# Two attention heads side by side on half arrays, bfloat16 masks, and one mask product for four mLSTM heads

## The chip, the core and the metric

The kernel runs on one core of one Trainium2 chip. The metric is the device time of one execution in microseconds (us), from three timed runs; one more execution was taken with the hardware profiler. TensorE (PE in the profile) does the matrix products, VectorE (DVE) and ScalarE (ACT) the elementwise work, GpSimd (POOL) and SyncE (SP) here issue transfers.

## What is computed

A batch of one with 256 tokens and 256 context tokens goes through a first block of two trunk layers (each a mixer with differential attention, and a gated feed-forward part) and then a second block (mLSTM in both directions beside a windowed attention with a sink, then a mixture of 16,384 small experts). Three places of the reference matter:

```python
def diff_attend(q, k, v, lam):                      # first block
    s = jnp.einsum('bqhmd,bkhmd->bhmqk', q, k).astype(jnp.float32) * (DIFF_QK ** -0.5)
    p = jax.nn.softmax(s, axis=-1)
    a = p[:, :, 0] - lam * p[:, :, 1]
    return jnp.einsum('bhqk,bkhd->bqhd', a.astype(v.dtype), v)
...
    log_d = jnp.where(seen, log_d, -jnp.inf)        # mLSTM, per head and chunk of 128
    m_t = jnp.maximum(log_inter, jnp.max(log_d, axis=-1))
    s = jnp.einsum('bhctk,bhcsk->bhcts', q, k) * jnp.exp(log_d - m_t[..., None])
...
    s_loc = jnp.where(mask[None, :, None, None], s_loc, -jnp.inf)   # windowed attention, 8 heads of 64
    p = _softmax_with_sink(jnp.concatenate([s_loc, s_ctx], axis=-1), sink_b)
```

## The kernel before, in words

Activations lie feature by token in SBUF. Each large product is written as three products of float32r halves: `weight` (lines 262 to 266) loads a weight tile of 128x1024 through SP into one of three `wraw` buffers, ACT casts it to `whi`, DVE subtracts to `wlo`; `gemm` (line 282) multiplies. One such tile against 256 tokens is 24 products of 256 columns. The order of instructions on each engine is written by a scheduler from the program order, priorities and a cost model; engines then run in that order.

**First block.** `mixer_d` works through steps `(seg, hp, hh, qt)`: queries of the tokens against 512 keys (seg 0) and, in layer 0 alone, queries of the context against 256 keys (seg 1); `hp` is a pair of heads, `hh` the head in it, `qt` a block of 128 queries. Layer 0 has 16 steps, layer 1 has 8. For a step, `scores` (lines 775 to 784) makes two products, two maxima, two exponentials and the weighted difference; `turned` (791, 793) transposes the result by up to four products with the identity into the one `pt` bank and ACT copies it to one of two `aT` buffers; `values` (800) multiplies each block of keys (4 or 2 of them) with the 64 columns of that head's values, writing to the 64 partitions `hh * 64` of `po` (`tile_position=(0, hh * 64)`: the left or the right half of the array's columns). Scores run two steps ahead, and after each step `next(fill)` puts in a piece of `mixer_fm`, the other products of the layer. Line 926 in `mixer_fm` already multiplies with both halves in turn.

**mLSTM.** `weights(tt, dd)`, called four times, builds for four heads a bank `pD`: per head a float32 product of a selector of 4 rows with a row of running maxima (line 1256), then a float32 product of the identity with a mask of 0 and 1e30 (1257). ACT takes four exponentials, DVE multiplies. `outputs` follows one turn later.

**Windowed attention.** `window_attention` has 16 steps `(i, qt, hh)`. `scores` (1382) multiplies 64 rows (a head's features, in partitions `hh * 64`: the upper or lower half of the array's rows) with 512 columns of keys, then adds the window's mask by a float32 product with the identity (1384); DVE takes the maximum (1387, 1388), ACT the exponential and the sink's (1391, 1392), DVE sums, inverts and scales (1393 to 1395). `turned` (1402, 1404) transposes by four products into `pt` and copies. Line 1419 multiplies with the values, in column halves. Scores run two steps ahead, and one of 16 products for the gates fills in after each step as long as there are any (five are used in the mLSTM).

A float32 product shows in the trace as two weight loads (PEld) and two MATMUL records; a float32r or 16-bit product as one of each. `self.att()` has four PSUM banks, `self.acc()` two, `pt` and `po` one each.

Of the kernel before, what the change touches and what calls it, by code (L numbers as in the profile page):

```python
# [11 lines left out]
F32 = mybir.dt.float32  # L12
F32R = mybir.dt.float32r
BF16 = mybir.dt.bfloat16
# [75 lines left out]
def second_constants():  # L90
    k = Pack()
    i = np.arange(P)
    k.add("tri_le", (i[:, None] <= i[None, :]).astype(np.float32))
    k.add("tri_ge", (i[:, None] >= i[None, :]).astype(np.float32))
    k.add("mask_le", np.where(i[:, None] <= i[None, :], 0.0, BIG))
    k.add("mask_ge", np.where(i[:, None] >= i[None, :], 0.0, BIG))
    k.add("win0", np.where(i[None, :] <= i[:, None], 0.0, -BIG))
    k.add("win1", np.where(i[None, :] >= i[:, None], 0.0, -BIG))
# [116 lines left out]
class Kernel:  # L215
# [472 lines left out]
    def mixer_d(self, l, mp, hi, lo, mix, lam, pva, fill, begin, later):  # L688
# [67 lines left out]
        self.lambdas(l, lam)  # L756
        gsub = self.sm([P, 1], "gsub", bufs=1)
        V.tensor_scalar(gsub, self.prm[f"subln{l}"], 1.0 - LAM_INIT[l], None, op0=OP.mult)
        steps = [(seg, hp, hh, qt) for seg in range(2 if full else 1) for hp in range(2) for hh in range(2) for qt in range(2)]
        span = lambda seg: (0, 1, 2, 3) if seg == 0 else (2, 3)  # L760
        ready = {}

        def scores(i):
            seg, hp, hh, qt = steps[i]
            k0, nk = span(seg)[0] * P, len(span(seg)) * P
            if seg and hh + qt == 0:
                for t in range(2):
# [25 lines left out]
            nc.scalar.copy(aT[:, :len(kts), :], pt[:, :len(kts) * P].rearrange("p (j t) -> p j t", t=P))  # L793
            return aT

        def values(i, aT, po):
            seg, hp, hh, qt = steps[i]
            h, kts = hp * 2 + hh, span(seg)
            for j, kt in enumerate(kts):
                nc.tensor.matmul(po[hh * 64:hh * 64 + 64, qt * P:qt * P + P], v[:, kt, h * 64:h * 64 + 64], aT[:, j, :], start=j == 0, stop=j == len(kts) - 1, tile_position=(0, hh * 64))  # L800

        def scaled(seg, ss, o_sb):
            r = self.rsqrt(ss.rearrange("p a b -> p (a b)"), [P, 8], "subr")
# [24 lines left out]
        fill = turns(fill)  # L828
        scores(0)
        scores(1)  # L830
        po, ss, o_sb = None, None, []
        for i, (seg, hp, hh, qt) in enumerate(steps):
            if hh + qt == 0:
                po = self.po()
            if hp + hh + qt == 0:
                ss, o_sb = self.sm([P, 2, 4], "subss", bufs=2), []
            if i == 8:
                later(2)
            aT = turned(i)
            if i + 2 < len(steps):  # L840
                scores(i + 2)
            for _ in range(1 if full else 2):
                next(fill, None)
            values(i, aT, po)
# [197 lines left out]
    def token_mixer(self):  # L1042
# [3 lines left out]
        with ExitStack() as st:  # L1046
# [11 lines left out]
            mT = (self.t(mp, [P, 4, TOK], F32R, "mT_hi"), self.t(mp, [P, 4, TOK], F32R, "mT_lo"))  # L1058
            aT = (self.t(mp, [P, 4, TOK], F32R, "aT_hi"), self.t(mp, [P, 4, TOK], F32R, "aT_lo"))
            ot = self.t(mp, [P, 4, TOK], F32, "o_th")  # L1060
            h = (hi[:, :, :TOK], lo[:, :, :TOK])

            def fm_tile(m):
# [39 lines left out]
    def mlstm(self, lp, mp, hi, lo, fm_tile, ot, mT, fill):  # L1103
# [264 lines left out]
        return kT, qT  # L1368

    def window_attention(self, lp, kT, qT, av, aT, fill):  # L1370
        nc, k, rows = self.nc, self.k, self.rows
        V = nc.vector
        nsink = self.sm([P, 8], "nsink", bufs=1)
        V.tensor_scalar(nsink, rows["sink"], -1.0, None, op0=OP.mult)
        steps = [(i, qt, hh) for i in range(4) for qt in range(2) for hh in range(2)]
        ready = {}

        def scores(n):
            i, qt, hh = steps[n]
            hd, r = i * 2 + hh, hh * 64  # L1380
            ps = self.att()
# [3 lines left out]
            mx = self.sm([P, 1], "wmx")  # L1385
            sk = rows["sink"][:, hd:hd + 1]
            V.tensor_reduce(mx, ps, axis=AX.X, op=OP.max, negate=True)
            V.tensor_tensor(mx, mx, nsink[:, hd:hd + 1], op=OP.min)
            e = self.t(lp, [P, 512], F32, "wexp", 3)
            sm = self.sm([P, 2], "wsm")  # L1390
            nc.scalar.activation(e, ps, AF.Exp, bias=mx, accum_out=sm[:, 0:1])
            nc.scalar.activation(sm[:, 1:2], sk, AF.Exp, bias=mx)
            V.tensor_tensor(sm[:, 0:1], sm[:, 0:1], sm[:, 1:2], op=OP.add)
            V.reciprocal(sm[:, 0:1], sm[:, 0:1])
            V.tensor_scalar(e, e, sm[:, 0:1], None, op0=OP.mult)
            ready[n] = e

        def turned(n):
            e = ready.pop(n)
# [3 lines left out]
            pT = self.t(lp, [P, 4, P], F32, "wpT", 2)  # L1403
            nc.scalar.copy(pT.rearrange("p a b -> p (a b)"), pt)
            return pT

        scores(0)
        scores(1)
        po = None
        for n, (i, qt, hh) in enumerate(steps):  # L1410
            if qt + hh == 0:
                po = self.po()
            pT = turned(n)
            if n + 2 < len(steps):
                scores(n + 2)
# [4 lines left out]
            if qt + hh == 2:  # L1420
                self.split(aT[0][:, i, :], aT[1][:, i, :], po[:, :TOK])
        for _ in fill:
            pass
# [298 lines left out]
```

## Time and profile before

| | |
|---|---|
| three timed runs | 2079.08, 2081.98, 2083.46 us (median 2081.98) |
| the profiled execution | 2075.71 us, of which the span from the first to the last instruction is 2073.9 us |
| instructions | 38449 |
| HBM read | 352.69 MB, 171 GB/s over the span |

Times in the rows further down are microseconds from the start of the span. A timeline row merges neighbours of one kind: its start, the time from the first start to the last end, and the count of records (xN). Ends of matmuls are modelled and overlap the next one, so what a piece of work takes on PE is read from the start of its row to the start of the next row. A row of stretches has the bounds, the length, the busy time (and instructions) of PE, PEld, DVE, ACT and POOL, the granted TensorE clock as a share of full speed, the DMA share and GB/s. A row of groups ends in: busy us, mean ns of one | idle us of the engine before them, and what ended it.

### The profile page before, as it was taken

How to read it: one execution, taken by the hardware profiler on the slowest of the kernel's cores; microseconds unless marked ns; L12 is line 12 of the kernel's file. 1: busy time of each engine (PE TensorE's matmuls, PEld its weight loads, DVE VectorE, ACT ScalarE, POOL GpSimd, SP SyncE). 2: the span in 40 equal slices, each digit the busy share in tenths (PEclk: the TensorE clock that was granted, in tenths of full speed). 3: DMA queues.
4: the chain of work that ended last, by engine and by line, in shares of the span. 5: the costliest groups of instructions: out<-in, count | busy, mean ns of one | idle time of the engine just before them, and what ended most of it. 6: DMA issues, size and time to landing. Idle time of an engine off the chain costs nothing. (4 is left out here: it accounts for less than half of the span.)

```text
span 2073.9 us, 38449 instructions
## 1 busy us (share of the span) xinstructions
PE 2010.9 (97%) x15084; PEld 1822.1 (88%) x15084; DVE 1675.6 (81%) x3484; ACT 987.2 (48%) x1681; POOL 71.0 (3%) x138
## 2 busy tenths in 40 slices
PE   7999999998999999999999999999999999999999
PEld 3777778887888889999798788999999999999999
DVE  5897889876976779987675479988987898898775
ACT  4476343322324856554344455456544444444444
POOL 0100001111110000000000000000000000000000
PEclk9999999999999999999999999999999999999999
DMA  7632346676663347774341253555465565555564
GB/s 284 214 113 70 132 153 213 224 245 221 215 211 122 103 132 257 262 249 132 103 144 61 77 148 123 162 182 166 146 189 187 179 186 186 179 181 191 183 190 157
DMA packets 99029, 356.23 MB, mean 172 GB/s; under 512 B 11296, under 2 KB 12192, under 8 KB 97312
## 3 DMA queue, kind: packets, MB, share of 16 engines
q1 hardware_dynamic: 77616, 279.21, 41.3%
q0 software_dynamic: 19296, 70.98, 10.3%
q10 hardware_dynamic: 1936, 3.59, 0.6%
q8 instruction: 118, 1.93, 0.4%
q14 instruction: 63, 0.52, 0.1%
HBM read 352.69 MB, written 1.05 MB: 171 GB/s over the span
## 5 line engine op out<-in xcount | busy, mean ns | idle before, releaser
L263 ACT CAST whi<-wraw 128x1024 fp32r<-128x1024 f32 (+2 forms) x524 | 537.8, 1028 | 407.0 <-PE pH L282 95.1
L266 DVE TENSOR_TENSOR wlo<-wraw,whi 128x1024 fp32r<-128x1024 f32 (+3 forms) x552 | 626.6, 1138 | 103.1 <-ACT whi L263 99.9
L1534 PE MATMUL out<-w_hi,whi 128*128 128x256 f32 x1024 | 284.0, 277 | 0.2 <-ACT w_hi L272 0.2
L1534 PE MATMUL out<-w_hi,wlo 128*128 128x256 f32 x1024 | 282.5, 276 | 0.0
L1534 PE MATMUL out<-w_lo,whi 128*128 128x256 f32 x1024 | 282.2, 276 | 0.0
L369 DVE SCALAR_TENSOR_TENSOR junk<-adaw,cvec 128x1024 bf16<-128x1024 f32 x192 | 234.4, 1221 | 49.8 <-DMA adaw<-ada_in 48.4
L1534 PEld LDWEIGHTS out<-w_hi,whi 128*128 128x128 f32 x1024 | 192.3, 188 | 0.3 <-ACT w_hi L272 0.3
L1534 PEld LDWEIGHTS out<-w_hi,wlo 128*128 128x128 f32 x1024 | 192.3, 188 | 0.1
L1534 PEld LDWEIGHTS out<-w_lo,whi 128*128 128x128 f32 x1024 | 192.0, 188 | 0.0
L282 PE MATMUL acc<-h_hi,whi 128*128 128x256 f32 (+1 forms) x880 | 169.8, 330 | 11.2 <-DVE xc L646 4.6
L282 PE MATMUL pH<-p_hi,whi 128*128 128x256 f32 x1128 | 160.4, 282 | 3.7 <-ACT act L1465 3.6
L272 ACT CAST w_hi<-act 128x256 fp32r<-128x256 f32 x128 | 51.9, 406 | 232.3 <-PE out L1534 223.8
L282 PE MATMUL acc<-h_lo,whi 128*128 128x256 f32 (+1 forms) x880 | 160.4, 322 | 0.0
L282 PE MATMUL acc<-h_hi,wlo 128*128 128x256 f32 (+1 forms) x880 | 159.3, 320 | 0.2 <-DVE wlo L266 0.2
L282 PEld LDWEIGHTS acc<-h_hi,whi 128*128 128x128 f32 x880 | 132.6, 193 | 27.0 <-issue 5.8
L282 PE MATMUL pH<-p_hi,wlo 128*128 128x256 f32 x1128 | 152.3, 277 | 0.1
L282 PE MATMUL pH<-p_lo,whi 128*128 128x256 f32 x1128 | 152.3, 277 | 0.0
L282 PEld LDWEIGHTS pH<-p_hi,whi 128*128 128x128 f32 x1128 | 140.7, 188 | 5.2 <-ACT act L1465 5.1
L282 PEld LDWEIGHTS acc<-h_hi,wlo 128*128 128x128 f32 x880 | 131.3, 189 | 13.7 <-DVE wlo L266 0.8
L282 PEld LDWEIGHTS acc<-h_lo,whi 128*128 128x128 f32 x880 | 132.0, 191 | 12.2 <-issue 0.3
L282 PEld LDWEIGHTS pH<-p_hi,wlo 128*128 128x128 f32 x1128 | 139.3, 188 | 0.3 <-DVE wlo L266 0.3
L282 PEld LDWEIGHTS pH<-p_lo,whi 128*128 128x128 f32 x1128 | 139.3, 188 | 0.0
(567 smaller groups left out, 3342.4 us busy)
## 6 DMA issues: line engine op xcount, KB each, us to landing
adaw<-ada_in POOLq DMA_DIRECT2D x128, 512.0 KB, 4.3
wraw<-pu_in SPq DMA_DIRECT2D x128, 512.0 KB, 3.5
wraw<-pv_in SPq DMA_DIRECT2D x128, 512.0 KB, 4.0
wraw<-wup_in SPq DMA_DIRECT2D x88, 512.0 KB, 4.4
wraw<-win_fm_in SPq DMA_DIRECT2D x44, 512.0 KB, 3.5
wraw<-wdn_in SPq DMA_DIRECT2D x32, 512.0 KB, 4.6
wraw<-wout_in SPq DMA_DIRECT2D x24, 512.0 KB, 3.6
adan<-ada0n_in SPq DMA_DIRECT2D x8, 1024.0 KB, 15.1
```

Source lines behind the costliest of these rows:

```text
L263: nc.scalar.copy(hi[:, :n], raw[:, :n])
L266: nc.vector.tensor_sub(lo[:, s], raw[:, s], hi[:, s].bitcast(F32))
L272: self.nc.scalar.copy(hi, src)
L282: nc.tensor.matmul(ps, a[:, k, :], b[:, k, :], start=first and j == 0, stop=last and j == len(todo) - 1)
L369: nc.vector.scalar_tensor_tensor(junk, w, 0.5, cv, op0=OP.mult, op1=OP.mult, accum_out=self.ada[key][:, nt:nt + 1])
L1534: nc.tensor.matmul(part(m), x[:, m, :], y, start=False, stop=False)
```

## The change

Four things. (1) In `mixer_d` the steps run as `(seg, hp, qt, hh)`, so that two heads with the same queries follow each other; the products with the values wait for both heads and alternate between the column halves. (2) In `weights` of the mLSTM one bfloat16 product of the identity with the mask, read four times over, covers all four heads; the four selector products follow it. (3) In `window_attention` a step is a pair of heads: score products of 256 columns alternate between the row halves, the masks are bfloat16, products with the values alternate between the column halves; scores run one pair ahead, `wexp` has 4 buffers for 3 and `wpT` 3 for 2. (4) The four float32 masks leave the table of constants (a transfer of 704 KB becomes 448 KB); the bfloat16 ones are made from `tri_le` and `tri_ge` by four DVE operations, and the identity by one ACT copy, at the start of the second block.

```diff
-    k.add("mask_le", np.where(i[:, None] <= i[None, :], 0.0, BIG))
...
-        steps = [(seg, hp, hh, qt) for seg in range(2 if full else 1) for hp in range(2) for hh in range(2) for qt in range(2)]
+        steps = [(seg, hp, qt, hh) for seg in range(2 if full else 1) for hp in range(2) for qt in range(2) for hh in range(2)]
...
-        def values(i, aT, po):
-            seg, hp, hh, qt = steps[i]
-            h, kts = hp * 2 + hh, span(seg)
+        def values(i, aTs, po):
+
+            seg, hp, qt, _ = steps[i]
+            kts = span(seg)
             for j, kt in enumerate(kts):
-                nc.tensor.matmul(po[hh * 64:hh * 64 + 64, qt * P:qt * P + P], v[:, kt, h * 64:h * 64 + 64], aT[:, j, :], start=j == 0, stop=j == len(kts) - 1, tile_position=(0, hh * 64))
+                for hh in range(2):
+                    h = hp * 2 + hh
+                    nc.tensor.matmul(po[hh * 64:hh * 64 + 64, qt * P:qt * P + P], v[:, kt, h * 64:h * 64 + 64], aTs[hh][:, j, :], start=j == 0, stop=j == len(kts) - 1, tile_position=(0, hh * 64))
...
-            aT = turned(i)
+            aTs.append(turned(i))
...
-            values(i, aT, po)
+            if hh == 1:
+                values(i, aTs, po)
+                aTs = []
...
+            k["ident_b"] = self.t(mp, [P, P], BF16, "ident_b")
+            nc.scalar.copy(k["ident_b"], k["ident"])
+            for n, tri, f in (("mask_le", "tri_le", -BIG), ("mask_ge", "tri_ge", -BIG), ("win0", "tri_ge", BIG), ("win1", "tri_le", BIG)):
+                k[n + "_b"] = self.t(mp, [P, P], BF16, n + "_b")
+                nc.vector.tensor_scalar(k[n + "_b"], k[tri], -1.0, f, op0=OP.add, op1=OP.mult)
...
+            mask = k[("mask_le_b", "mask_ge_b")[dd]]
+            nc.tensor.matmul(pD.rearrange("p (h t) -> p h t", h=4), k["ident_b"], mask.unsqueeze(1).to_broadcast([P, 4, P]), start=True, stop=False)
             for hd in range(4):
-                o = pD[:, hd * P:hd * P + P]
-                nc.tensor.matmul(o, k["sel4"][0:4, hd * P:hd * P + P], Mr[dd][:, tt, :], start=True, stop=False)
-                nc.tensor.matmul(o, k["ident"], k[("mask_le", "mask_ge")[dd]], start=False, stop=True)
+                nc.tensor.matmul(pD[:, hd * P:hd * P + P], k["sel4"][0:4, hd * P:hd * P + P], Mr[dd][:, tt, :], start=False, stop=hd == 3)
...
-        steps = [(i, qt, hh) for i in range(4) for qt in range(2) for hh in range(2)]
+        steps = [(i, qt) for i in range(4) for qt in range(2)]
...
-            nc.tensor.matmul(ps, qT[r:r + 64, i, qt * P:qt * P + P], kT[r:r + 64, hd // 4, :], start=True, stop=False, tile_position=(r, 0))
...
-            nc.tensor.matmul(ps[:, o:o + P], k["ident"], k[f"win{qt}"], start=False, stop=True)
...
+            for half in (1, 0):
+                for hh in range(2):
+                    r, g = hh * 64, (i * 2 + hh) // 4
+                    c = slice(half * TOK, half * TOK + TOK)
+                    nc.tensor.matmul(ps[hh][:, c], qT[r:r + 64, i, qt * P:qt * P + P], kT[r:r + 64, g, c], start=True, stop=half == 1, tile_position=(r, 0))
+            for hh in range(2):
+                nc.tensor.matmul(ps[hh][:, o:o + P], k["ident_b"], k[f"win{qt}_b"], start=False, stop=True)
...
+            pT = [turned(n, 0)]
+            if n + 1 < len(steps):
+                scores(n + 1)
             next(fill, None)
-            g, r = (i * 2 + hh) // 4, hh * 64
+            pT.append(turned(n, 1))
+            next(fill, None)
             for j in range(4):
-                nc.tensor.matmul(po[r:r + 64, qt * P:qt * P + P], av[:, j, g * 64:g * 64 + 64], pT[:, j, :], start=j == 0, stop=j == 3, tile_position=(0, r))
+                for hh in range(2):
+                    g, r = (i * 2 + hh) // 4, hh * 64
+                    nc.tensor.matmul(po[r:r + 64, qt * P:qt * P + P], av[:, j, g * 64:g * 64 + 64], pT[hh][:, j, :], start=j == 0, stop=j == 3, tile_position=(0, r))
```

## Rows read from the trace of the kernel before

**Rows 1.** Page, part 1: busy time, share of the span and instructions of each engine.

```profile
PE 2010.9 (97%) x15084; PEld 1822.1 (88%) x15084; DVE 1675.6 (81%) x3484; ACT 987.2 (48%) x1681; POOL 71.0 (3%) x138
```

**Rows 2.** Stretches: layer 0, layer 1, part of the mLSTM, window, experts.

```profile
104.00:207.00 103.00, 101.56 (x549) 79.78 (x548) 87.57 (x215) 69.59 (x170) 4.23 (x8) 1.00 0.27 91
703.00:742.00 39.00, 37.29 (x276) 32.44 (x275) 31.04 (x77) 31.91 (x75) 0.03 (x1) 1.00 0.25 81
1090.00:1101.00 11.00, 11.00 (x45) 9.21 (x45) 2.27 (x6) 3.66 (x12) 0.00 (x0) 0.53 0.04 15
1130.00:1207.00 77.00, 76.81 (x493) 57.66 (x492) 39.04 (x103) 39.74 (x95) 0.00 (x0) 1.00 0.20 65
1264.00:2073.00 809.00, 799.46 (x7869) 791.38 (x7867) 687.41 (x1327) 394.42 (x590) 0.00 (x0) 1.00 0.56 175
```

**Rows 3.** Timeline of PE, one step of the window with fill.

```profile
1160.98 1.09 PE L1419 MATMUL po<-wpT,av 128*64 128x128 f32 x8
1161.99 0.66 PE L1402 MATMUL pt<-consts,wexp 128*128 128x128 f32 x4
1162.58 1.12 PE L1382 MATMUL att<-akT,aqT 64*128 64x512 f32 x2
1163.63 0.49 PE L1384 MATMUL att<-consts,consts 128*128 128x128 f32 x2
1163.88 1.20 PE L282 MATMUL acc<-h_hi,whi 128*128 128x256 f32 x8
...
1166.91 1.09 PE L1419 MATMUL po<-wpT,av 128*64 128x128 f32 x8
```

**Rows 4.** Timeline of PE, column halves in turn, then one half alone.

```profile
181.83 1.09 PE L926 MATMUL acc<-wsT,va 128*64 128x128 f32 x16
182.75 0.60 PE L800 MATMUL po<-aT,vtm 128*64 128x128 f32 x4
```

**Rows 5.** Timeline of PE, the window's first scores and first transposes.

```profile
1130.15 1.12 PE L1382 MATMUL att<-akT,aqT 64*128 64x512 f32 x2
...
1139.42 0.60 PE L1402 MATMUL pt<-consts,wexp 128*128 128x128 f32 x4
```

**Rows 6.** Timeline of PE, 16-bit products in the expert stage.

```profile
1503.89 0.64 PE L1503 MATMUL pg<-ohg,oh 128*128 128x64 f16 x16
1504.36 0.81 PE L282 MATMUL pH<-p_hi,whi 128*128 128x256 f32 x5
```

**Rows 7.** Groups of ACT and DVE in the window, 1130 to 1207.

```profile
L1387 DVE TENSOR_REDUCE wmx<-att 128x1 f32<-128x512 f32 x16 | 11.1, 691 | 19.3 <-PE att L1384 19.2
L1395 DVE TENSOR_SCALAR wexp<-wexp,wsm 128x512 f32<-128x512 f32 x16 | 7.8, 485 | 0.5
L1391 ACT ACTIVATE wexp<-att,wmx 128x512 f32<-128x512 f32 x16 | 11.0, 689 | 10.5 <-DVE wmx L1388 9.6 <-DVE wsm L1394 0.9
L1404 ACT COPY wpT<-pt 128x512 f32<-128x512 f32 x16 | 9.4, 587 | 17.8 <-PE pt L1402 17.8
L1392 ACT ACTIVATE wsm<-rows,wmx 128x1 f32<-128x1 f32 x16 | 4.6, 288 | 1.0 <-DVE wmx L1388 0.8 <-DVE wsm L1394 0.2
```

**Rows 8.** Timeline of PE, `weights` in the mLSTM: two turns, then one.

```profile
1087.03 0.48 PE L1256 MATMUL att<-Mrow,consts 4*128 4x128 f32 x2
...
1096.13 0.64 PE L1274 MATMUL att<-mC,mqT 128*128 128x129 f32 x2
...
1101.29 0.48 PE L1256 MATMUL att<-Mrow,consts 4*128 4x128 f32 x2
1101.71 0.49 PE L1257 MATMUL att<-consts,consts 128*128 128x128 f32 x2
1102.13 0.48 PE L1256 MATMUL att<-Mrow,consts 4*128 4x128 f32 x2
...
1104.53 0.39 PE L1274 MATMUL att<-mC,mqT 128*128 128x129 f32 x2
```

**Rows 9.** The transfer of the second table of constants, line 314.

```profile
L314 POOL DMA_DIRECT2D consts<-consts_in x1: 527/527/527, 900.3 to 900.3; - x1
```

More of the change, by code (lines that the diff above doesn't have):

```diff
@@ L94, in second_constants @@
     k.add("tri_ge", (i[:, None] >= i[None, :]).astype(np.float32))
-    k.add("mask_le", np.where(i[:, None] <= i[None, :], 0.0, BIG))
-    k.add("mask_ge", np.where(i[:, None] >= i[None, :], 0.0, BIG))
-    k.add("win0", np.where(i[None, :] <= i[:, None], 0.0, -BIG))
-    k.add("win1", np.where(i[None, :] >= i[:, None], 0.0, -BIG))
     k.add("sel4", np.kron(np.eye(4), np.ones((1, P))))
@@ L763, in scores @@
         def scores(i):
-            seg, hp, hh, qt = steps[i]
+            seg, hp, qt, hh = steps[i]
             k0, nk = span(seg)[0] * P, len(span(seg)) * P
@@ L794, in turned @@
             return aT
-        def values(i, aT, po):
-            seg, hp, hh, qt = steps[i]
-            h, kts = hp * 2 + hh, span(seg)
+        def values(i, aTs, po):
+            seg, hp, qt, _ = steps[i]
+            kts = span(seg)
             for j, kt in enumerate(kts):
-                nc.tensor.matmul(po[hh * 64:hh * 64 + 64, qt * P:qt * P + P], v[:, kt, h * 64:h * 64 + 64], aT[:, j, :], start=j == 0, stop=j == len(kts) - 1, tile_position=(0, hh * 64))
+                for hh in range(2):
+                    h = hp * 2 + hh
+                    nc.tensor.matmul(po[hh * 64:hh * 64 + 64, qt * P:qt * P + P], v[:, kt, h * 64:h * 64 + 64], aTs[hh][:, j, :], start=j == 0, stop=j == len(kts) - 1, tile_position=(0, hh * 64))
         def scaled(seg, ss, o_sb):
@@ L830, in mixer_d @@
         scores(1)
-        po, ss, o_sb = None, None, []
-        for i, (seg, hp, hh, qt) in enumerate(steps):
+        po, ss, o_sb, aTs = None, None, [], []
+        for i, (seg, hp, qt, hh) in enumerate(steps):
             if hh + qt == 0:
@@ L1374, in window_attention @@
         V.tensor_scalar(nsink, rows["sink"], -1.0, None, op0=OP.mult)
-        steps = [(i, qt, hh) for i in range(4) for qt in range(2) for hh in range(2)]
+        steps = [(i, qt) for i in range(4) for qt in range(2)]
         ready = {}
         def scores(n):
-            i, qt, hh = steps[n]
-            hd, r = i * 2 + hh, hh * 64
-            ps = self.att()
-            nc.tensor.matmul(ps, qT[r:r + 64, i, qt * P:qt * P + P], kT[r:r + 64, hd // 4, :], start=True, stop=False, tile_position=(r, 0))
+            i, qt = steps[n]
+            ps = [self.att() for _ in range(2)]
@@ L1383, in scores @@
             o = (1 - qt) * P
-            nc.tensor.matmul(ps[:, o:o + P], k["ident"], k[f"win{qt}"], start=False, stop=True)
[L1385 to L1399, printed above, removed]
+            for half in (1, 0):
[3 more added lines that the diff above has]
+                    nc.tensor.matmul(ps[hh][:, c], qT[r:r + 64, i, qt * P:qt * P + P], kT[r:r + 64, g, c], start=True, stop=half == 1, tile_position=(r, 0))
@@ new lines, in scores @@
+            for hh in range(2):
+                nc.tensor.matmul(ps[hh][:, o:o + P], k["ident_b"], k[f"win{qt}_b"], start=False, stop=True)
+            for hh in range(2):
+                hd = i * 2 + hh
+                mx = self.sm([P, 1], "wmx")
+                sk = rows["sink"][:, hd:hd + 1]
+                V.tensor_reduce(mx, ps[hh], axis=AX.X, op=OP.max, negate=True)
+                V.tensor_tensor(mx, mx, nsink[:, hd:hd + 1], op=OP.min)
+                e = self.t(lp, [P, 512], F32, "wexp", 4)
+                sm = self.sm([P, 2], "wsm")
+                nc.scalar.activation(e, ps[hh], AF.Exp, bias=mx, accum_out=sm[:, 0:1])
+                nc.scalar.activation(sm[:, 1:2], sk, AF.Exp, bias=mx)
+                V.tensor_tensor(sm[:, 0:1], sm[:, 0:1], sm[:, 1:2], op=OP.add)
+                V.reciprocal(sm[:, 0:1], sm[:, 0:1])
+                V.tensor_scalar(e, e, sm[:, 0:1], None, op0=OP.mult)
+                ready[n, hh] = e
@@ L1400, in turned @@
+        def turned(n, hh):
+            e = ready.pop((n, hh))
             pt = self.pt()
@@ L1402, in turned @@
                 nc.tensor.transpose(pt[:, j * P:j * P + P], e[:, j * P:j * P + P], k["ident"])
-            pT = self.t(lp, [P, 4, P], F32, "wpT", 2)
+            pT = self.t(lp, [P, 4, P], F32, "wpT", 3)
             nc.scalar.copy(pT.rearrange("p a b -> p (a b)"), pt)
@@ L1407, in window_attention @@
         scores(0)
-        scores(1)
         po = None
-        for n, (i, qt, hh) in enumerate(steps):
-            if qt + hh == 0:
+        for n, (i, qt) in enumerate(steps):
+            if qt == 0:
                 po = self.po()
-            pT = turned(n)
-            if n + 2 < len(steps):
-                scores(n + 2)
+            pT = [turned(n, 0)]
+            if n + 1 < len(steps):
+                scores(n + 1)
             next(fill, None)
-            g, r = (i * 2 + hh) // 4, hh * 64
+            pT.append(turned(n, 1))
+            next(fill, None)
             for j in range(4):
-                nc.tensor.matmul(po[r:r + 64, qt * P:qt * P + P], av[:, j, g * 64:g * 64 + 64], pT[:, j, :], start=j == 0, stop=j == 3, tile_position=(0, r))
-            if qt + hh == 2:
+                for hh in range(2):
+                    g, r = (i * 2 + hh) // 4, hh * 64
+                    nc.tensor.matmul(po[r:r + 64, qt * P:qt * P + P], av[:, j, g * 64:g * 64 + 64], pT[hh][:, j, :], start=j == 0, stop=j == 3, tile_position=(0, r))
+            if qt == 1:
                 self.split(aT[0][:, i, :], aT[1][:, i, :], po[:, :TOK])
```

## The prediction

> **What bounds the kernel now.** I read the page first: PE is busy for 97% of the span [rows 1]. Since a modelled busy time can hide waiting, I then cut the span by stage [rows 2]. In the two attention stages of the first block, in the mLSTM and in the window PE is busy for 96 to 100% of each stretch, while in the window DVE and ACT are busy for only 39 and 40 of 77 us. After the window come the merge and then 809 us of experts, PE busy 99%. So time taken off PE in an early stage should simply move everything after it forward. Last I read the timeline of PE in the window [rows 3], to see what a step is made of, from start to start: products with the values 1.01 us, transposes 0.59, scores 1.05, mask 0.25, one fill tile 3.03. No gap is left that another engine would have to close. PE's own work is the price of a step there.
>
> **The window.** It has 16 such steps.
>
> Values: eight records of one half take 1.01 us [rows 3]. Line 926 already alternates the halves: its 16 records take 0.92 us, 0.058 each, where the four records of one half behind them take 0.53 [rows 4]. Two halves in turn thus run beside each other, and a pair of heads costs what one head cost. 16 x 1.01 becomes 8 x 1.01, which saves 8.1 us.
>
> Scores: no row shows the two row halves in turn, so this is bounded. If they run beside each other as the column halves do, 16 x 1.05 becomes 8 x 1.05 and saves 8.4. If not, and each change of half costs what a change of array layout costs, the saving turns into a loss: eight value records take 1.01 and four 0.53 [rows 3, 4], so four more cost 0.48, 0.12 each, while two records between changes take 0.41 [rows 8], so a change costs some 0.17, say 0.2. A pair has two changes now; with one before each of its eight records of half the length it would lose 6 x 0.2 = 1.2, 9.6 in all. I take 8.4, since the nearest row is that of line 926. The Trainium skill (TensorE: Matmul & The Clock Gate, Measured speedup vs the span model) gives 3.07 times for four row tiles, 77% of the ideal; by that two halves would give 1.54 times, the scores would save 5.9 for 8.4 and the whole sum below would be 30 for 32.5; no row here has it.
>
> Masks: 0.25 us [rows 3] to 0.42 (line 1257, which has the same form [rows 8]), on average some 0.29, times 16 is 4.7. A 16-bit product of 64 columns takes 0.47 / 16 = 0.029 [rows 6], so 128 columns take 0.06; two of them and 0.1 of the 0.17 that separates 0.42 from 0.25 make 0.2 a pair, 1.7 in all. Saved: 3.0.
>
> Together 19.5 us, if PE never waits. It will: the cover goes in two places. At the start, 9.3 us lie between the first scores and the first transposes [rows 5], set by the exponentials and what precedes them; five score steps and 2.1 us of fill stood there, now two pairs of 2.5 us stand there and some 1.5 fill tiles more are used up early. At the end there is then no fill for about three of the eight pairs. A pair without fill has 3.3 us of PE work, but its next transposes need a maximum (0.69), an exponential (0.69), the sink's (0.29) and the scaling (0.49) [rows 7] in line behind the scores, some 2.9 with the small operations, so a pair lasts about 0.5 + 1.25 + 2.9 = 4.7. That is 1.4 lost three times, 4.5 with the first hand-over through the single `pt` bank. **Window: -15 us.** Bounds: -19.5 if PE never waits; -3 if a pair's whole chain ran without overlap, 8 us for each of eight pairs behind 9.3 us of start.
>
> **The mLSTM.** A block of `weights` takes 1101.29 to 1104.53, 3.24 us [rows 8]: eight times 0.41, with a change of layout between the four-row product and the full one each time. After: one 16-bit product of 512 columns, 0.029 x 8 = 0.23 [rows 6], and a change, 0.1 to 0.2; then eight records in one layout, as the eight of line 1419, 1.01, and a little for the first load. That is 1.4, and 4 x 1.85 = 7.4 us saved at full clock. DVE and ACT do not bind here, as 2.3 and 3.7 us of 11 show [rows 2]; what `outputs` waits for is covered by the fill tile of each turn. If that cover failed, each turn would wait up to the four exponentials and the multiply, 2 us. The granted clock is 0.53 between 1090 and 1101 [rows 2], that is at 1.2 GHz for some 10 of 11 us, after three microseconds of four-row products; the first two blocks took 9.1 us for 6.5 because of it [rows 8]. Fewer such products stand there afterwards. Whether the clock then holds is open: it gives back between 0 and 5 us, and I take 2.6. **mLSTM: -10 us.** Bounds: -5 (waits come in, the clock stays) and -12.5.
>
> **The first block.** In layer 0 eight steps have eight value records (1.01 us) and eight have four (0.53 to 0.58, [rows 4]); pairs halve that: 4.1 + 2.2 = 6.3. In layer 1 eight steps of 1.01 give 4.1. PE has no slack in layer 0, but DVE is at 87.6 of 103 us [rows 2] and would be at 91%; with both near full I count 60% of 6.3, 3.8, and 3.7 of 4.1. Pairs now hold both `aT` buffers, so the copy for the next step waits for the products of this pair; these stand ahead of its transposes on PE, hence nothing is paid; with that order lost it is one copy, 0.59 [rows 7], for 12 pairs, 7 us, which would eat the gain. **First block: -7.5 us.** Bounds: 0 and -10.5.
>
> **Small edits.** The four mask operations on DVE and the copy on ACT cost at most 4 x 0.49 + 0.59 = 2.5 us, the price of four times their columns [rows 7]; their source is issued at 900 us [rows 9], 187 us before the first use, so no engine stands waiting for it, and on PE's path they cost nothing. Were that cover gone, it would be those 2.5 us. The table's transfer shrinks by 256 KB, with nothing timed behind it.
>
> **Sum.** 15 + 10 + 7.5 = 32.5 us off the profiled execution's 2075.7, so 2043.2. That execution is 6.3 below the median of the three runs; the forecast is for such a median: 2082.0 - 32.5 = 2049.5, given as 2049.
>
> **Rivals.**
>
> (a) The halves do not run beside each other where no row shows it, the row halves. For: all rows of line 1382 have one half between changes of layout. Against: the column halves do it [rows 4], and the two heads write to different banks. The window's scores then save nothing or lose up to 9.6; the sum is 24 down to 14.5, the time 2058 to 2067. If even the value products failed to overlap, the change would not do what it says and only the masks would be left, about 13.
>
> (b) Emptying PSUM becomes the bound. Pairs bring two exponentials, two maxima and two copies at once to ACT and DVE; ACT needs at least 689 + 288 + 587 ns a head, 3.1 us a pair [rows 7], nearly the 3.3 of PE, and DVE in layer 0 is at 85% already [rows 2]. Against: with fill, a pair in the window lasts 9 us. Taken to the end the window saves 5, the mLSTM 6, the first block 2: 13, time 2069. The Trainium skill (TensorEngine Tiling, PSUM Bottleneck) states just this, that the copy out of PSUM may become the limit once tiling speeds up TensorE; the half-empty DVE and ACT of the window speak against it there.
>
> (c) Slower: TensorE's clock falls to 1.2 GHz in the window. Stretches with partial arrays and waits stand before the slow part of the mLSTM [rows 2, 8]; with waits of 1 to 2 us in its pairs the window might look alike. After the change it holds 57 us of PE work at full clock (31 of fill, 26 of attention), so all of it at half clock costs 57: 32.5 - 57 = 24 slower, 2106. It decides from 33 us of work at half clock on. Against: the same half-array products ran there at 1.00 for 77 us.
>
> **How the numbers follow.** Forecast 0.74, (a) 0.11, (b) 0.11, (c) 0.04. With the clock given back whole, no waits and the full 10.5 of the first block, the low end is 19.5 + 12.5 + 10.5 = 42.5, and some 6 us are left for other slow stretches and run-to-run difference: 2033. The high end takes in (a) and most of (b): 2070. A measurement of this kernel can tell about 0.2%, 4.2 us, from no change. Faster by more than that: the forecast, (a) and most of (b), 0.92; within: the rest of (b) and weak forms of (c), 0.04; slower 0.04.
>
> **What would show it.** In the changed profile, right steps look like this: value records in pairs at 0.06 us each, 16 in some 1.0 us; a pair's scores in about 1.05 us; a block of `weights` in 1.4; the window shorter by 15 and PE there below 97% busy, with waits on ACT or DVE in its last pairs; the experts still 809 us. Wrong: scores of 1.9 us or more a pair (a); PE with gaps in every pair or in layer 0, and DVE near 95% (b); a granted clock well under 1 between 1100 and 1200 (c); or an expert stage whose length changes, which would mean the order written by the scheduler shifted work that I count as untouched.

## The result, and the profile after

The changed kernel takes 2048.19 us (median of four runs, 2045.21 to 2054.14), the kernel before beside it 2082.72 (four runs, 2079.08 to 2083.70). By the medians that is 34.5 us (1.66%) less. The ratio taken over all the runs is 0.9845 with an interval of 0.9826 to 0.9864, that is 28 to 36 us less. The forecast was 2049. The profiled execution of the changed kernel took 2045.4 us, its span 2043.6.

Part 1 of the page, which answers to [rows 1]:

```profile
PE 1979.9 (97%) x15072; PEld 1804.8 (88%) x15072; DVE 1673.9 (82%) x3488; ACT 985.5 (48%) x1682; POOL 71.1 (3%) x138
```

PE has lost 31.0 us of busy time and only twelve instructions. Its share of the span is still 97%: the time went out of PE's own work, and no other engine has taken over.

The view of stretches, as [rows 2], for the same four stages of the changed kernel (layer 0, layer 1, the start of the mLSTM, the window):

```profile
104.00:203.00 99.00, 97.46 (x553) 76.07 (x552) 87.75 (x219) 69.04 (x170) 4.22 (x8) 1.00 0.29 96
703.00:742.00 39.00, 36.70 (x283) 30.59 (x282) 31.97 (x82) 33.65 (x79) 0.00 (x0) 1.00 0.26 82
1085.00:1100.00 15.00, 14.90 (x101) 13.41 (x102) 8.09 (x30) 7.86 (x23) 0.00 (x0) 0.89 0.22 70
1118.00:1178.00 60.00, 59.55 (x514) 50.90 (x514) 38.76 (x105) 38.25 (x94) 0.00 (x0) 1.00 0.28 85
```

The window is 60 us long where it was 77, with PE as full as before and DVE and ACT busy for 39 and 38 us. DVE in layer 0 is at 89% of the stretch. The start of the mLSTM has a granted clock of 0.89, that is 1.2 GHz for some 3 of its 15 us, where [rows 2] had 0.53 over 11 us. In the changed kernel the fall comes at 1089.3, just behind the first two blocks of `weights`; in the kernel before it came at 1090.3, when only the first block was done, so that the whole second block ran at 1.2 GHz.

The timeline of PE in the window, to be read from start to start as [rows 3]: its first two pairs, a pair that has fallen apart, a whole pair with its scores, and one of the last pairs.

```profile
1118.02 1.49 PE L1393 MATMUL att<-akT,aqT 64*128 64x256 f32 x8
1119.44 0.29 PE L1395 MATMUL att<-win_b,ident_b 128*128 128x128 bf16 x2
1119.54 0.36 PE L278 MATMUL acc<-h_hi,whi 128*128 128x256 f32 x1
...
1126.79 0.43 PE L1434 MATMUL po<-wpT,av 128*64 128x128 f32 x2
1127.16 1.10 PE L278 MATMUL acc<-h_hi,whi 128*128 128x256 f32 x7
1128.18 1.09 PE L1434 MATMUL po<-wpT,av 128*64 128x128 f32 x14
1129.20 0.66 PE L1415 MATMUL pt<-consts,wexp 128*128 128x128 f32 x4
...
1150.81 1.09 PE L1434 MATMUL po<-wpT,av 128*64 128x128 f32 x16
1151.83 0.66 PE L1415 MATMUL pt<-consts,wexp 128*128 128x128 f32 x4
1152.42 1.14 PE L1393 MATMUL att<-akT,aqT 64*128 64x256 f32 x8
1153.49 0.29 PE L1395 MATMUL att<-win_b,ident_b 128*128 128x128 bf16 x2
1153.58 1.19 PE L278 MATMUL acc<-h_hi,whi 128*128 128x256 f32 x8
...
1170.14 0.43 PE L1434 MATMUL po<-wpT,av 128*64 128x128 f32 x2
1170.51 0.74 PE L278 MATMUL acc<-mT_hi,whi 128*128 128x256 f32 x4
1171.18 1.09 PE L1434 MATMUL po<-wpT,av 128*64 128x128 f32 x14
```

Three readings. The 16 value records of a pair take 1.02 us (1150.81 to 1151.83), what eight took for one head. The eight score records of a pair, on row halves, take 1.07 (1152.42 to 1153.49), what one head's two records of twice the length took. And at 1126.79 a pair has come apart, because the scheduler put other products between its parts: two records alone, 0.37 us, seven records of fill, then the other fourteen, which still take 1.02. This happens in five of the eight pairs, 0.36 us each time.

Adding the records of the window from start to start gives the balance, from the start of the first score record to the start of the last value record (us):

| | before | after | difference |
|---|---|---|---|
| scores | 16.84 | 9.68 | -7.2 |
| values | 16.09 | 9.77 | -6.3 |
| masks | 4.65 | 0.82 | -3.8 |
| transposes | 7.94 | 7.50 | -0.4 |
| fill and products of the merge | 31.08 | 32.11 | +1.0 |
| first scores to last values | 76.6 | 59.9 | -16.7 |

The waits of the weight loads there, as engine, tile and line, who was waited for, total, times and longest (us), come to little:

```profile
PEld po L1434 <- ACT wpT L1417: 0.8, 3, 0.3
PEld att L1393 <- ACT mnum L1319: 0.6, 2, 0.3
PEld pt L1415 <- DVE wexp L1408: 0.5, 1, 0.5
```

The second row is new work for a pair: it takes two `att` banks at once, and the second one was still being read by the last activations of the mLSTM (line 1319). It shows in the first two pairs, whose scores took 1.42 us (1118.02 to 1119.44).

The timeline of PE in the mLSTM, two blocks of `weights` behind each other, as the start of [rows 8]:

```profile
1085.59 0.38 PE L1261 MATMUL att<-mask_le_b,ident_b 128*128 128x512 bf16 x1
1085.90 1.15 PE L1263 MATMUL att<-Mrow,consts 4*128 4x128 f32 x8
1086.98 0.39 PE L1261 MATMUL att<-mask_ge_b,ident_b 128*128 128x512 bf16 x1
1087.31 1.16 PE L1263 MATMUL att<-Mrow,consts 4*128 4x128 f32 x8
1088.39 0.49 PE L1280 MATMUL att<-mC,mqT 128*128 128x129 f32 x2
```

A block takes 1085.59 to 1086.98, 1.39 us, of which the mask is 0.31. From the first block's start to the transposes of the output the stage takes 30.9 us for 41.6. (Two expectations further down count it from the first selector product, which now stands behind the mask: 30.6.)

The timeline of PE in the first block, the first two pairs of layer 0, and a place late in layer 1 where PE waits:

```profile
120.43 0.43 PE L799 MATMUL po<-aT,vtm 128*64 128x128 f32 x2
120.79 1.20 PE L278 MATMUL acc<-h_hi,whi 128*128 128x512 f32 x4
121.83 0.39 PE L278 MATMUL acc<-h_lo,whi 128*128 128x512 f32 x1
122.14 1.09 PE L799 MATMUL po<-aT,vtm 128*64 128x128 f32 x14
...
133.66 1.09 PE L799 MATMUL po<-aT,vtm 128*64 128x128 f32 x16
```

```profile
737.67 0.38 PE L799 MATMUL po<-aT,vtm 128*64 128x128 f32 x2
737.98 0.66 PE L787 MATMUL pt<-consts,e 128*128 128x128 f32 x4
739.31 0.66 PE L787 MATMUL pt<-consts,e 128*128 128x128 f32 x4 [0.68 <-ACT aT L789]
```

Pairs fall apart here too (120.43, 122.14). In layer 1 the transposes of the two heads now stand directly behind each other, and the second set waits 0.68 us for ACT to empty the single `pt` bank. From the first transposes of layer 0 to the first transfer for its output weight the changed kernel takes 18.8 us for 23.8; the rest of layer 0's mixer, up to the first product of the feed-forward part, 100.9 for 100.7; layer 1, from the first value product to the end of the mixer, 41.6 for 43.3.

So the altered stages give 4.9 + 1.7 + 10.7 + 16.7 = 34.0 us. The two profiled executions differ by 30.3 only, because the stages that the change does not touch were together 3.7 us shorter in the profiled execution of before, which at 2075.7 us lies below all the timed runs shown of it.

### The profile page after: what moved, and what is told of

The parts are those of the page before. It is cut to its first block, busy times and chain, and to the rows that moved or that the text cites. A ratio compares the mean times of both kernels' runs of the same rounds, so it can differ in the third digit from the quotient of the medians.

```text
span 2043.6 us, 38424 instructions
## 1 busy us (share of the span) xinstructions
PE 1979.9 (97%) x15072; PEld 1804.8 (88%) x15072; DVE 1673.9 (82%) x3488; ACT 985.5 (48%) x1682; POOL 71.1 (3%) x138
## 3 DMA queue, kind: packets, MB, share of 16 engines
HBM read 352.42 MB, written 1.05 MB: 173 GB/s over the span
## 5 line engine op out<-in xcount | busy, mean ns | idle before, releaser
L262 DVE TENSOR_TENSOR wlo<-wraw,whi 128x1024 fp32r<-128x1024 f32 (+3 forms) x552 | 628.2, 1141 | 102.4 <-ACT whi L259 100.7
```

The costliest lines, as they stand in the source:

```text
L262: nc.vector.tensor_sub(lo[:, s], raw[:, s], hi[:, s].bitcast(F32))
```

## The experiments

Times are compared with runs of the kernel before on the same chip: 2082.82 us (median) for the first four experiments, 2082.38 for the next four, 2083.14 for the last two. The stage lengths are taken between the same marks as above.

**Each part alone.** Three kernels are the one before with one part of the change put in: the order of heads and the pairs of `values` in `mixer_d`; the mask product in `weights`; the pairs and masks of `window_attention`. Each keeps the float32 masks that it still reads in the table.

```diff
# first block alone
-        steps = [(seg, hp, hh, qt) for seg in range(2 if full else 1) for hp in range(2) for hh in range(2) for qt in range(2)]
+        steps = [(seg, hp, qt, hh) for seg in range(2 if full else 1) for hp in range(2) for qt in range(2) for hh in range(2)]
...
-            values(i, aT, po)
+            if hh == 1:
+                values(i, aTs, po)
# mLSTM alone
+            nc.tensor.matmul(pD.rearrange("p (h t) -> p h t", h=4), k["ident_b"], mask.unsqueeze(1).to_broadcast([P, 4, P]), start=True, stop=False)
# window alone
-        steps = [(i, qt, hh) for i in range(4) for qt in range(2) for hh in range(2)]
+        steps = [(i, qt) for i in range(4) for qt in range(2)]
```

First block:

> Only the first block's attention is changed (pairs of heads, values alternating between column halves); the rest is the kernel before. Theory (time is what leaves PE, and the first block's stages have no other bound): layer 0's attention ends about 4 us earlier, layer 1's about 2 us, and 6 us show at the end: ratio about 0.997. Rival (given back: what is gained in layer 0 is lost again in its feed-forward part, whatever the cause): the last transfers of the feed-forward part of layer 0 start at the same time as before within 1 us, and the time is the same within 2 us.

mLSTM:

> Only the mLSTM's masks are changed (one 16-bit product for four heads, then four selector products). Theory: a block of weights takes 1.4 us for 3.24, the mLSTM is 10 us shorter, the time 10 us less (ratio 0.995). Rival (waits of outputs and the latency of its chain take the room): 5 us or less.

Window:

> Only the windowed attention is changed. Theory: the window takes 60 us for 77 and the time is 17 us less (ratio 0.992), the same as in the whole change, because the parts do not share a resource. Rival (the parts help each other, for instance through the clock): the window alone brings under 12 or over 22 us.

| | median us (ratio, interval) | its own stage | other altered stages |
|---|---|---|---|
| first block | 2078.30 (0.9978, 0.9962 to 0.9994) | 18.8 and 41.6 | 41.5 and 76.6, as before |
| mLSTM | 2069.22 (0.9927, 0.9900 to 0.9954) | 30.9 | 23.8, 43.3 and 76.6, as before |
| window | 2062.51 (0.9904, 0.9882 to 0.9927) | 59.9 | 23.8, 43.3 and 41.5, as before |

Each part gives in its own stage what the whole gives there, to 0.1 us, and nothing in the other altered ones. By medians they save 4.5, 13.6 and 20.3 us, 38.4 together for 34.5 of the whole, the same within their intervals. The parts are independent, as they must be if PE's work is the price of each stage.

One sign of a rival did come. In the profile of the first block's kernel the last transfer of layer 0's feed-forward part starts at 615.06 us, for 614.34 before, within the 1 us that the rival named. But this part is not the same length in two executions of the same instructions. From its first transfer to its last it took 377.4 us in the profile of before, and 382.2 and 378.9 in the mLSTM's and the window's kernel, whose first block is that of before; in the first block's kernel it took 381.3. So the profile of before was at the short end there, and the twelve timed runs, 4.5 us less with an interval of 1.2 to 8, lean to the theory.

**Head after head.** All of the change, but the products of a pair are put out one head after the other: the loop over `hh` becomes the outer one in `values` of the first block, in the window's scores and in its values.

```diff
-            for half in (1, 0):
-                for hh in range(2):
+            for hh in range(2):
+                for half in (1, 0):
```

> The whole change, but the halves do not alternate: for each pair all products of the first head stand before all of the second, for values in the first block and the window and for scores in the window. Theory (products of different halves run beside each other only because they alternate in the queue): PE loses the overlap, a pair's 16 value records take 1.9 us for 1.03 and its scores 1.9 for 1.07; 7 + 7 us come back in the window and 5 in the first block, so about 19 us slower than the whole change (ratio to the kernel before about 0.993). Rival (the gain comes from fewer changes of array layout, or the engine pairs the halves by itself): within 4 us of the whole change (ratio 0.985).

Measured: 2061.86 us (0.9892, 0.9866 to 0.9918), the window 62.7, layer 0 19.5, layer 1 42.9. The timeline of PE in that window, a pair's values and the next pair's scores, then a later pair's values:

```profile
1144.85 1.58 PE L1434 MATMUL po<-wpT,av 128*64 128x128 f32 x16
1146.36 0.66 PE L1415 MATMUL pt<-consts,wexp 128*128 128x128 f32 x4
1146.95 1.14 PE L1393 MATMUL att<-akT,aqT 64*128 64x256 f32 x8
1148.02 0.28 PE L1395 MATMUL att<-win_b,ident_b 128*128 128x128 bf16 x2
...
1180.39 1.85 PE L1434 MATMUL po<-wpT,av 128*64 128x128 f32 x16
1182.17 0.66 PE L1415 MATMUL pt<-consts,wexp 128*128 128x128 f32 x4
```

My theory fell, and the time lies between it and the rival. The scores of a pair take 1.07 us in this order as well: single records show the second head's first weight load 12 ns after the first head's. The values take 1.51 in the four whole pairs where both copies were ready, between the 1.02 of the alternating order and twice that: five records of the first head run alone, then the second head's start. So the engine takes instructions of the other half forward by itself, over a limited distance; what counts is that both halves' work stands close together, and alternating is worth 0.5 us of such a value pair. Two more whole pairs take 1.78 (1180.39 to 1182.17) and 1.82, because ACT's copy for the second head ended only then: its first weight load comes 0.05 us after the copy's end, with seven records of the first head already started. The scheduler parted the other two. All values of the window take 13.66 us for 9.77.

The window lost 2.8 us, the first part of layer 0 0.7, the rest of its mixer, which holds the later pairs, 2.8 (103.7 for 100.9), layer 1 1.3: 7.6 in all. Of the 2.8 in the rest of the mixer some 1.7 are the clock, whose mean was 0.95 there for 0.97. By medians it is 13.7 us slower than the changed kernel, by the profiled executions 18.4. The clock can account for most of what the stages leave: a mean clock of 0.983 over 2062.0 us for 0.989 over 2043.6 is about 70 us at 1.2 GHz for 46, and if all of it delays the end, some 12 us. That is an estimate from the two traces. Why the clock was lower in this execution is not shown.

**Which part of the window pays what.** The changed kernel once more, unaltered, beside three edits: the second head's product first in `values` (first block and window), the window's values of each head by themselves, and the window's mask of the first head between the two heads' scores.

```diff
# late head first
-                for hh in range(2):
+                for hh in (1, 0):
# values apart
-            pT = [turned(n, 0)]
...
+            for hh in range(2):
+                pT = turned(n, hh)
...
+                for j in range(4):
+                    nc.tensor.matmul(po[r:r + 64, qt * P:qt * P + P], av[:, j, g * 64:g * 64 + 64], pT[:, j, :], start=j == 0, stop=j == 3, tile_position=(0, r))
# mask between
-            for half in (1, 0):
-                for hh in range(2):
+            for hh in range(2):
+                for half in (1, 0):
...
-            for hh in range(2):
                 nc.tensor.matmul(ps[hh][:, o:o + P], k["ident_b"], k[f"win{qt}_b"], start=False, stop=True)
```

> The changed kernel once more, unaltered, for a second profile and more times. If the 5.6 us that its first profile lost in layer 0's feed-forward part against the profile before belong to the change, this profile loses them again in the same stage; if they are differences between executions (stretches at 1.2 GHz that move), the stage is some us shorter or longer here and the ratio to the kernel before stays at 0.983 to 0.986.

> The changed kernel with the two heads of a pair in the other order in the products with the values (head 1, whose copy comes last, first). Theory (the pair falls apart in the order of PE because head 0's first product is let go ahead alone, at 0.36 us each time; with the late head first all products stand behind it): groups of 16 records at 1.03 us stay whole in the window, values there take 8.3 us for 10.0, so the window is 1.5 us shorter, the attention of layers 0 and 1 together up to 2 us; 2 to 4 us less in all, ratio to the kernel before about 0.983. Rival (the early product filled a wait, so nothing is gained, or head 1's late copy now stops PE): the window within 0.5 us of the changed kernel's 59.9 or longer.

> The changed kernel, but in the window the products with the values stand apart again, each head's four behind its own transposes, so that other products lie between the halves. Theory (two halves overlap only within a group): 16 groups of 8 records at 1.02 us, values 16.3 us for 10.0, the window 6 us longer (66), the time 6 us more. Rival (the saving in the window lies in scores and masks): the window under 62.

> The changed kernel, but in the window the 16-bit mask product of the first head stands between the scores of the first and of the second, a product of the full array between the two row halves. Theory (the row halves overlap when they stand together, and not across a product of the full array): scores of a pair take 2.1 us for 1.07, the masks a little more, the window 8 to 9 us longer (68), the time 8 us more. Rival (the row halves did not overlap; 1.07 comes from shorter products): within 2 us of 59.9.

| | median us (ratio, interval) | window | scores, values, masks |
|---|---|---|---|
| unaltered | 2050.59 (0.9865, 0.9842 to 0.9887) | 59.9 | 9.68, 9.78, 0.81 |
| late head first | 2049.12 (0.9860, 0.9836 to 0.9883) | 57.9 | 9.84, 8.00, 0.77 |
| values apart | 2056.45 (0.9891, 0.9863 to 0.9918) | 67.6 | 10.00, 16.09, 0.87 |
| mask between | 2057.55 (0.9889, 0.9857 to 0.9921) | 67.3 | 17.35, 9.78, 1.61 |

In the unaltered kernel's second profile layer 0's feed-forward part, from its first transfer to its last, took 380.3 us, for 382.9 in the first and 377.4 before. It was shorter by 2.6 without any edit, so what the first profile had lost there is at least in part a difference between executions. The ratio lies at 0.9865, just above the range that was named.

The timeline of PE in the window, "late head first", then "values apart", then "mask between":

```profile
1165.74 1.09 PE L1434 MATMUL po<-wpT,av 128*64 128x128 f32 x16
1166.76 0.66 PE L1415 MATMUL pt<-consts,wexp 128*128 128x128 f32 x4
```

```profile
1148.13 1.09 PE L1432 MATMUL po<-wpT,av 128*64 128x128 f32 x8
1149.15 0.66 PE L1415 MATMUL pt<-consts,wexp 128*128 128x128 f32 x4
```

```profile
1147.35 1.13 PE L1393 MATMUL att<-akT,aqT 64*128 64x256 f32 x4
1148.41 0.23 PE L1394 MATMUL att<-win_b,ident_b 128*128 128x128 bf16 x1
1148.57 1.13 PE L1393 MATMUL att<-akT,aqT 64*128 64x256 f32 x4
1149.63 0.23 PE L1394 MATMUL att<-win_b,ident_b 128*128 128x128 bf16 x1
```

In "mask between" a full product stands between the halves. Four records of one head then take 1.06 us, as long as eight of both, and the window's scores are back at 17.35, near the 16.84 of before. Row halves beside each other are thus worth 17.35 - 9.68 = 7.7 us here, and the masks, each with a change of form of its own, cost 0.8 more; fill took 1.1 less, so that the window is 7.4 longer. "Values apart" prices the column halves: with each head's products at its own place the values cost the 16.09 of before, 16.09 - 9.78 = 6.3 us more. "Late head first" mends the falling apart: a pair's first product is now the one whose `wpT` comes last, so the scheduler has no reason to put it out early, all eight pairs are whole, and the values take 8.00, as 8 x 1.0 should. Its window is 2.0 us shorter for 1.5 expected, and layer 0's mixer 1.2 shorter, but layer 1 is 0.5 longer from its first transposes to its last value product. Its total, 1.5 below the unaltered one, cannot be told from it, so the 2 to 4 us less in all did not show. So no version here is shown to beat the changed kernel.

**The mLSTM's mask: type or grouping.** In one kernel each head has a bfloat16 mask product of its own again, behind its selector product; in the other the one product for four heads stays, in float32.

```diff
# mask per head, bfloat16
-            nc.tensor.matmul(pD.rearrange("p (h t) -> p h t", h=4), k["ident_b"], mask.unsqueeze(1).to_broadcast([P, 4, P]), start=True, stop=False)
...
+                nc.tensor.matmul(o, k["sel4"][0:4, hd * P:hd * P + P], Mr[dd][:, tt, :], start=True, stop=False)
+                nc.tensor.matmul(o, k["ident_b"], mask, start=False, stop=True)
# one mask for four heads, float32
-            mask = k[("mask_le_b", "mask_ge_b")[dd]]
-            nc.tensor.matmul(pD.rearrange("p (h t) -> p h t", h=4), k["ident_b"], mask.unsqueeze(1).to_broadcast([P, 4, P]), start=True, stop=False)
+            mask = k[("mask_le_f", "mask_ge_f")[dd]]
+            nc.tensor.matmul(pD.rearrange("p (h t) -> p h t", h=4), k["ident"], mask.unsqueeze(1).to_broadcast([P, 4, P]), start=True, stop=False)
```

> The changed kernel, but in weights of the mLSTM each head has its own bfloat16 mask product again, behind its selector product: the changes between the four-row form and the full one are back, the masks stay 16-bit. My theory: most of the 7.4 us saved at full clock comes from the eight changes of form that are gone, not from fewer columns; a block of weights then takes 4 x (0.41 + some 0.2) = 2.4 to 2.9 us for the 1.39 of the changed kernel and the 3.24 of the kernel before, the stage from the first selector product to the transposes of its output 34 to 37 us for 30.6, the whole 4 to 7 us over the changed kernel. Rival: the saving is the 16-bit mask alone; the block then stays at 1.6 or less and the stage within 1 us of 30.6.

> The changed kernel, but the mLSTM mask that is read four times over stays float32, with the float32 identity: one product of 512 columns in two records. My theory: the grouping alone keeps most of the gain. The window's float32 product of 512 columns took 1.05 us in the kernel before; by that the block takes 1.05 + 1.08 = 2.1 for 1.39, the stage 33.5 for 30.6, the whole 3 us over the changed kernel, 8 under the kernel before in this stage. Rival: the type carries the gain; the block then lies near 3.24 and the stage near 41.6.

The mask per head: 2054.98 us (0.9859, 0.9834 to 0.9884), the stage 37.3 for 30.9. The timeline of PE over its first block, of which the last line begins the second block, and the stretch of the stage:

```profile
1088.41 0.48 PE L1263 MATMUL att<-Mrow,consts 4*128 4x128 f32 x2
1088.83 0.23 PE L1264 MATMUL att<-mask_le_b,ident_b 128*128 128x128 bf16 x1
1088.99 0.48 PE L1263 MATMUL att<-Mrow,consts 4*128 4x128 f32 x2
...
1090.71 0.48 PE L1263 MATMUL att<-Mrow,consts 4*128 4x128 f32 x2
```

```profile
1088.00:1126.00 38.00, 37.58 (x246) 33.49 (x246) 21.94 (x74) 17.94 (x45) 0.00 (x0) 0.87 0.23 77
```

The float32 group: 2053.74 us (0.9858, 0.9831 to 0.9886), the stage 32.0 (31.1 from the first selector product, for 33.5 expected). The same two views:

```profile
1092.00 1.02 PE L1262 MATMUL att<-mask_le_f,consts 128*128 128x512 f32 x2
1092.96 1.15 PE L1264 MATMUL att<-Mrow,consts 4*128 4x128 f32 x8
1094.04 1.13 PE L1262 MATMUL att<-mask_ge_f,consts 128*128 128x512 f32 x2
```

```profile
1093.00:1124.00 31.00, 30.62 (x230) 27.48 (x229) 20.53 (x73) 16.87 (x44) 0.00 (x0) 1.00 0.24 79
```

A block takes 2.30 us with a bfloat16 mask per head and 2.04 with one float32 mask for four, between the 3.24 of before [rows 8] and 1.39. Neither edit carries the gain alone: the type saves 0.94 of the 1.85 us, the grouping the other 0.91; taken the other way round, grouping saves 1.20 and the type 0.65. "Most of it by the grouping" was too much. The stages show the clock on top. With one float32 mask no part of the stage ran below full clock: the four blocks cost 4 x 0.65 = 2.6 us more, the 1.7 us that the changed kernel loses to the clock there fall away, and the stage is 1.2 longer. With a mask per head the clock of the stretch was 0.87, a loss of 0.13 x 38 = 4.9 us for 1.7; with 4 x 0.91 = 3.6 for the blocks that makes 6.8, and the stage is 6.4 longer.

## Why the prediction was right

The path was right: PE's own work bounds the early stages, and everything after them moved forward; the experts took 805.2 us for 805.8. The sum was 32.5 us, by stages it is 34.0, by medians 34.5. That it came so close is in part luck: the stages were off by 1.7, 0.7 and 0.9 us, and inside them larger errors cancelled.

- **Window, -15 forecast, -16.7 measured.** "Column halves in turn run beside each other" was right at 1.02 us a pair, and the bounded step, that row halves do the same, took its upper end: 1.07 for two heads. The Trainium skill (TensorE: Matmul & The Clock Gate, Measured speedup vs the span model) gives 3.07 times for four row tiles. This trace does better with two halves, 2 x 1.05 for 1.07, that is 1.96 times of 2 possible; the measurement decides here. Three sizes and the cover were off and nearly cancelled, which is luck. Values gave 6.3 where 8.1 was counted: the step "a pair costs what one head cost" leaves out that an order written by a scheduler may start a pair as soon as its first product is ready; turning the two heads round gave the missing 1.8. Scores gave 7.2 for 8.4, since the first two pairs waited for an `att` bank and the transposes behind the third for their scaling. Masks gave 3.8 for 3.0, as a pair of them takes 0.10 us for 0.2 assumed.
- **The failed step of the window is the cover, 4.5 us.** I wrote that at the end there is no fill for three pairs, so PE waits. The last pairs have fill: `acc<-mT_hi` at 1170.51 is a product of the merge, which the scheduler draws forward, and fill in the window even grew by 1.0 us. PE is busy for 99% of the window, where below 97% was named as the sign, and its loads waited for other engines 2.2 us in all in the three groups above and one of 0.3. Two small readings of that sum were low as well: 2.3 us of fill, not 2.1, stood ahead of the first transposes, and the pieces named for a pair add up to 3.4 us of PE work, not 3.3. I had counted only the gates' sixteen tiles as cover and had not looked at what already stood in the tail of the window before, as this row of its timeline of PE shows:

```profile
1199.50 0.72 PE L282 MATMUL acc<-mT_hi,whi 128*128 128x256 f32 x4
```

- **mLSTM, -10 forecast, -10.7 measured.** The block of 1.4 us came out at 1.39. The blocks give 4 x 1.85 = 7.4; the remaining 3.3 are the clock's: at half speed, 0.47 x 11 = 5.2 us were lost in the stretch of before and 0.11 x 15 = 1.7 now, some 3.5 given back where I took 2.6. The reason that I gave was half of it: changes of layout are worth 0.91 of the 1.85, the 16-bit type the rest.
- **First block, -7.5 forecast, -6.6 measured**, with the parts the other way round. Layer 0 gave 4.9 of a possible 6.3 where I counted 3.8: DVE at 89% did not bind, and PE waited for it 0.3 us in 99. Layer 1 gave 1.7 where I counted 3.7, and here the step "nothing is paid" for the two `aT` buffers failed in part: value products gave 2.1 of 4.1, and transposes took 0.9 and scores 0.6 more. The transposes of two heads meet in one `pt` bank, and ACT's copy between them shows as a wait of 0.68.
- **Small edits** cost nothing that shows: the four mask operations take 0.22 us each on DVE and the copy 0.28 on ACT, 926 to 931 us into the span and some 155 us ahead of the first use, so the cover that the prediction named was there.
- **Rivals.** (a) fell with the scores at 1.07. (b) did not come: in the window DVE and ACT are busy for 39 and 38 of 60 us. The Trainium skill (TensorEngine Tiling (Array Packing), PSUM Bottleneck) says that the copy out of PSUM may become the limit once TensorE is faster. This trace does not show it: PE's waits for such copies are 1.7 us in layer 1 and 0.5 in layer 0, the same as before. (c) did not come: the window ran at 1.00.

## What to carry to other kernels

Where products use half of the array, put the other half's products next to them: a pair then costs what one cost, as long as no full product stands between. Count what a scheduler will do with the group: let it begin with the operand that comes last, which was worth 2.0 us in the window's stage here, though not to be seen in the total. Two members of a pair that share a bank can wait for each other, as the transposes of layer 1 did for 0.68 us; a bank for each was not tried. Where small products with few rows alternate with full ones, price the change of form and the type of the full one separately, since each was worth about half here.

## What was not expected

The order within a pair matters less to TensorE than I expected. With one head's records wholly ahead of the other's, eight score records still took 1.07 us, and sixteen value records 1.51 for 1.02 where both operands were ready, because work of the second half began before the first half's was done.

The total moves by more than the smaller edits are worth, and the granted clock is only a part of that. In one set of runs the unaltered changed kernel has spans from 2043.5 us at a mean clock of 0.988 to 2055.4 at 0.985, and the kernel before 2074.5 at 0.988 to 2083.2 at 0.984. But in the set of the result two executions of the changed kernel took 2043.4 us at 0.987 and 2052.4 at 0.988, so the mean clock does not put them in order. The stretches at 1.2 GHz come to some 41 us in the profile of "values apart" and to 70 in that of "head after head". They stand partly at other places in each profile, and in stages that no edit touches, so an edit of 2 us was to be seen in its stage and not in the total. What sets them in those stages was not tried and stays open, as does the rest of the difference between executions.
